# Hybrid encoder block: weight blocks of the value groups cast and reduced apart over a second load queue, and filter and forward-transform products in float32r parts

## Chip, core and metric

The kernel runs on one core of a Trainium2 chip. The metric is the time of one execution on the device, in microseconds (us). A difference below about 0.2% can't be told from no change.

## The reference

One layer on x of 512 positions by 2048 channels, in float32:

```
mod = silu(c) @ w_ada + b_ada            # shift1, scale1, gate1, shift2, scale2, gate2: 6 x 2048
h   = x * (1 + scale1) + shift1
z   = h @ w_in + b_in                    # 2048 x 9216: u, v | Hyena v, x1, x2 | gates a, b
A   = gelu(u) * (W_s @ LN(gelu(v)) + b_s)          # per chunk of 128 positions, 8 groups
B: z_h = short_conv3(z_h); v, x1, x2 = split(z_h)  # 3 x 1024 channels
   y = v
   for n, gate in enumerate((x1, x2)):             # two long convolutions
       y = gate * (irfft(rfft(y, 2L) * spectrum(filter_n)) + y * skip_n)
mix = (sigmoid(a) * (A @ w_a) + sigmoid(b) * (B @ w_b)) @ w_o + b_o
x   = LN(alpha * x + gate1 * mix)
x   = LN(alpha * x + gate2 * (relu(x * (1 + scale2) + shift2) @ w1 + b1)**2 @ w2 + b2)
```

The filters come from a small network: two sines, a product with `w3`, an exponential window. Forward and backward filter together form one two-sided kernel, whose spectrum multiplies that of the signal.

## The kernel before

**Dense products.** Every weight matrix is stored as blocks of 128 x 1024 float32 (512 KB), each holding two slices of 128 inputs by 512 outputs. A block is loaded into one of three `wraw` buffers (`Weights.load`, L120), cast by ScalarE (ACT) to float32r as `whi` (L76), and VectorE (DVE) takes the remainder `wlo` = `wraw` - `whi` (L77). The activations are kept as the same kind of pair. A product is three float32r matmuls, high by high, high by low and low by high (L187), so a block costs 24 matmuls of 128x512. A column group of 512 outputs over 2048 inputs is 8 blocks. `Weights.prepare` (L140) emits cast and remainder together and asks for the next load on SyncE's queue (SP); `take` (L153) calls it ahead of each block, so that one or two blocks are ready ahead of TensorE (PE).

The program is emitted in the order of the Python code, and every engine and queue works through its own part strictly in that order. An instruction that waits holds everything behind it on its engine.

**Start and filters.** SP's queue is asked first for `cond` (c broadcast to all partitions), then for blocks of `w_ada`; ScalarE's queue for the small tables of the filter network (L221 to L224). The rows of `w_ada` lie on partitions, and one step `ada.step` (L263) on DVE multiplies a block of 128x1024 by silu(c) and sums along the row. A slice of 128 of the modulation's shift1 and scale1 takes 4 such steps; `first_input` (L423) then makes one slice of the input pair `h1`: two sums on GpSimd (POOL), two activations on ACT (L428, L429), the remainder on POOL (L430). All of `h1` is 64 steps. A step also asks for the next `w_ada` block; nine or so are in buffers or under way.

Meanwhile the filters' spectra are made in eight parts `n` (L494). For each: `taps(n+1)`, four float32 products of the network's last layer with `w3` (L387, and L389 for the skip term in every second part); `transform(n)`, six float32 products with a table `fwd` of cosines and sines (L321, L325, L333); on DVE two `ada` steps, four products with the window (L397), and six sums (`sums`, L337 to L342). The spectra go to device memory (`store`, L401), apart from those of one convolution half, which stay.

**The value groups.** The loop of L516 computes column groups 4 and 5 of `w_in` (the Hyena `v`) together, slice by slice, since `h1` comes only as fast as the `ada` steps. Per pass `kp` of eight it prepares blocks, runs `ada` steps in fours until `h1` is three slices ahead (`LEAD`), and then runs one block of each group on PE. It is the order of this loop that sets how DVE, ACT, POOL and SP follow each other. I call it the value stage.

**Convolutions.** Column groups 6 to 9 give the gates x1 and x2. Between their blocks the convolutions run as `stages`, a table that says after which block which piece is emitted: transposes to tokens (`to_tokens`, L535), forward transforms (`Conv.odd`, L550, and `Conv.even`, L565, eight float32 products of 128x512 per convolution half and eight sums or more on DVE), six products with the spectrum per quarter (`times`, L577), folds (L587), the inverse (L613, L622). `into`, `between`, `out_of` and `last` (L642 to L677) are these tables. There are two convolutions of two halves of 512 channels each. A ring of eight PSUM banks serves all products.

After that come the remaining groups of `w_in`, `w_b`, `w_a`, `w_o` and the MLP, which the change leaves alone.

## Time and profile before

| | us |
|---|---|
| median of 3 runs | 2764.24 (2763.06 to 2766.48) |
| profiled execution | 2763.92 |
| its span in the trace | 2762.1 |
| start, to the first windowed filter part | 0 to 30.6 |
| filter parts | 30.6 to 98.7 |
| value stage on PE | 98.65 to 212.6 |
| groups 6 to 9, gates and convolutions | 212.6 to about 500 |
| the rest | to 2762.1 |

The page gives busy time per engine, queues and groups of instructions. In a row of a timeline the columns are start, duration, engine, line, operation, output and inputs, the number of instructions joined in the row, and in brackets the idle time ahead with what ended it. In a row of waits they are who waited, for whom, us in total, times, and the longest. In a row of stretches each engine's busy time is followed by its instruction count in brackets, and then come the clock that TensorE was granted, the share of the DMA engines, and GB/s.

### The profile page before, as it was taken

The numbers are of one execution on the slowest core, as the hardware profiler recorded it, in microseconds if no ns is written. First come the engines' busy times: TensorE is split into PE (matmuls) and PEld (weight loads), VectorE is DVE, ScalarE is ACT, GpSimd is POOL, SyncE is SP. The second block draws the span as 40 slices with busy tenths as digits, with TensorE's granted clock in tenths as the row PEclk, the third lists the DMA queues.
The fourth block names the chain that finished last, engine by engine and source line by source line (L and its number), as shares of the span: only waits on it lengthen the run. The fifth ranks groups of instructions, "written<-read, shape, count | busy, mean of one in ns | idle before, by whom it ended". The sixth has DMA issues, their size and how long they took to land.

```text
span 2762.1 us, 29764 instructions
## 1 busy us (share of the span) xinstructions
PE 2703.0 (98%) x11917; PEld 2199.8 (80%) x11917; DVE 1519.6 (55%) x2026; ACT 768.4 (28%) x932; POOL 109.3 (4%) x104
## 2 busy tenths in 40 slices
PE   7989999999999999999999999999999999999996
PEld 3667777888888888887988888888888888888885
DVE  7866968644566657546774343343433433434348
ACT  2234322322222222314631221312213122131232
POOL 1120000000000000050020000000000000000001
PEclk9989999999999999999999999999999999999998
DMA  8672332555665568454552222332222232223242
GB/s 321 241 293 82 127 102 99 190 193 191 201 207 191 185 202 287 139 185 163 167 163 96 99 92 101 98 99 94 97 99 94 97 99 98 94 92 107 93 143 77
DMA packets 120474, 400.46 MB, mean 145 GB/s; under 512 B 14219, under 2 KB 14315, under 8 KB 120208
## 3 DMA queue, kind: packets, MB, share of 16 engines
q1 hardware_dynamic: 119880, 398.20, 42.4%
q8 instruction: 93, 1.52, 0.2%
q10 hardware_dynamic: 456, 0.37, 0.0%
q14 instruction: 45, 0.37, 0.0%
HBM read 388.01 MB, written 10.50 MB: 144 GB/s over the span
## 4 chain that ended last, share of the span: by engine, by line
PE 88%; DVE 4%; DMA 1%; ACT 1%; issue 1%; POOL 0%; SPq 0%; DVEq 0%; ACTq 0%
PE d L187 56%; PE t L874 28%; PE inv L628 1%; DVE wlo L77 1%; PE inv L616 0%; DMA araw<-in_ada 0%; DMA wraw<-in_w_m 0%; DVE r L1026 0%; DVE r L890 0%; PE tr L539 0%; DVE r L1028 0%; PE h2T L914 0%; PE mix L750 0%; PE f L558 0%; PE f L556 0%
## 5 line engine op out<-in xcount | busy, mean ns | idle before, releaser
L187 PE MATMUL d<-act,whi 128*128 128x512 f32 (+1 forms) x4224 | 1285.1, 387 | 15.9 <-POOL act L430 9.0
L77 DVE TENSOR_TENSOR wlo<-wraw,whi 128x1024 fp32r<-128x1024 f32 x480 | 590.3, 1233 | 1030.7 <-ACT whi L76 1027.7
L76 ACT CAST whi<-wraw 128x1024 fp32r<-128x1024 f32 x480 | 504.5, 1054 | 1534.6 <-PE d L187 919.2
L187 PEld LDWEIGHTS d<-act,whi 128*128 128x128 f32 x4224 | 786.7, 189 | 181.3 <-POOL act L430 10.7
L187 PE MATMUL d<-act,wlo 128*128 128x512 f32 (+1 forms) x2112 | 811.9, 384 | 1.8 <-DVE wlo L77 1.8
L187 PEld LDWEIGHTS d<-act,wlo 128*128 128x128 f32 x2112 | 398.5, 189 | 81.7 <-DVE wlo L77 3.5
L874 PE MATMUL t<-whi,fh 128*128 128x512 f32 x960 | 373.4, 389 | 0.0
L874 PE MATMUL t<-wlo,fh 128*128 128x512 f32 x960 | 373.4, 389 | 0.0
L874 PE MATMUL t<-whi,fl 128*128 128x512 f32 x960 | 373.4, 389 | 0.0
L263 DVE SCALAR_TENSOR_TENSOR araw<-araw,cond 128x1024 f32<-128x1024 f32 x192 | 230.3, 1219 | 11.0 <-DMA araw<-in_ada 10.9
L874 PEld LDWEIGHTS t<-whi,fh 128*128 128x128 f32 x960 | 180.2, 188 | 37.5
L874 PEld LDWEIGHTS t<-wlo,fh 128*128 128x128 f32 x960 | 180.2, 188 | 37.4
L874 PEld LDWEIGHTS t<-whi,fl 128*128 128x128 f32 x960 | 180.2, 188 | 37.4
L874 PE MATMUL t<-whi,act 128*128 128x512 f32 x512 | 160.9, 393 | 0.0
L874 PEld LDWEIGHTS t<-whi,act 128*128 128x128 f32 x512 | 96.8, 189 | 20.4
L889 DVE TENSOR_TENSOR gated<-t,cond 128x512 f32<-128x512 f32 x126 | 86.2, 684 | 31.6 <-PE t L874 31.6
L874 PE MATMUL t<-wlo,act 128*128 128x512 f32 x256 | 100.4, 392 | 2.1 <-DVE wlo L77 2.1
L890 DVE TENSOR_TENSOR r<-r,gated 128x512 f32<-128x512 f32 x126 | 87.2, 692 | 4.4
L187 PE MATMUL d<-whi,act 128*128 128x512 f32 x256 | 79.0, 389 | 0.0
L984 DVE TENSOR_TENSOR relu<-relu 128x512 f32<-128x512 f32 (+1 forms) x68 | 45.6, 671 | 38.2 <-ACT fh L983 38.2
L1028 POOL TENSOR_TENSOR r<-r,ln2b 128x512 f32<-128x512 f32 x6 | 10.0, 1662 | 1306.0 <-DVE r L1026 1304.7
L874 PEld LDWEIGHTS t<-wlo,act 128*128 128x128 f32 x256 | 48.5, 189 | 12.3 <-DVE wlo L77 2.5
(220 smaller groups left out, 1886.1 us busy)
## 6 DMA issues: line engine op xcount, KB each, us to landing
wraw<-in_w_m SPq DMA_DIRECT2D x264, 512.0 KB, 3.4
araw<-in_ada SPq DMA_DIRECT2D x192, 512.0 KB, 4.9
wraw<-in_w_in SPq DMA_DIRECT2D x144, 512.0 KB, 3.5
wraw<-in_w_o SPq DMA_DIRECT2D x48, 512.0 KB, 3.9
spec<-spec SPq DMA_DIRECT2D x48, 256.0 KB, 4.0
wraw<-in_w_b SPq DMA_DIRECT2D x16, 512.0 KB, 3.6
wraw<-in_w_a SPq DMA_DIRECT2D x16, 512.0 KB, 3.9
xT<-in_xT SPq DMA_DIRECT2D x16, 256.0 KB, 6.4
```

The costliest lines, as they stand in the source:

```text
L76: nc.scalar.copy(hi, src)
L77: nc.vector.tensor_tensor(lo, src, f32(hi), op=OP.subtract)
L187: nc.tensor.matmul(out[i], a, b, start=first and m == 0, stop=last and m == 2)
L263: nc.vector.scalar_tensor_tensor(raw, raw, 1.0, cond[:, 1024 * h:1024 * (h + 1)], op0=OP.mult, op1=OP.mult, accum_out=dots[:, m, kc, h:h + 1])
L628: nc.tensor.matmul(ps[:, cl * P:(cl + 1) * P], conv.y[cl][cs][:, s], ic(4 * cs + COLUMN[cl]), start=(cs == 0), stop=(cs == 1))
L874: nc.tensor.matmul(out[i], a, b, start=kc == 0 and m == 0, stop=kc == 2 * pairs - 1 and m == 2)
L889: nc.vector.tensor_tensor(x, ps[i], g2_row[c], op=OP.mult)
L890: nc.vector.tensor_tensor(r[i][c], r[i][c], x, op=OP.add)
L984: nc.vector.tensor_tensor(x, x, x, op=OP.mult)
L1028: eng.tensor_tensor(x, x, ln2_b[c], op=OP.add)
```

## The change

Four things are changed.

1. In `Weights`, cast and remainder can be emitted apart (`cast`, `finish`), and a load asked for later (`later`, `flush`). From the filter parts to the end of the value stage the weight blocks are loaded over ScalarE's queue. The loop of the value stage goes by 16 half passes `u` of one block each: ask for the loads held back, 3 or 4 `ada` steps, the remainder of the next block, PE's block, the cast of the one after. All 64 `ada` steps are done by the thirteenth half pass.
2. The filters' last layer (`taps`) and the convolutions' forward transforms (`angle_product`) use float32r pairs in three matmuls in place of one float32 product. Pairs are made of `w3`, of the second sine's output `a2`, of the table `fwd` (after the value stage), and of the tokens. The filter parts' own transforms stay in float32.
3. The tables of stages move some pieces by one block (`late`, and `even(0)` of the second convolution into the next group).
4. At the start, the first two small tables are asked for on SP's queue, `cond` comes in two loads, the +1 on the scales moves from POOL to DVE, and 38 transposes of the identity into a bank that nothing reads (`busy`) are put on PE between the first products.

The order of the instructions moves at three places on which the prediction rests. In the rows, a name's number tells its buffers apart.

First, VectorE in the value stage, about a third of the way through. `wlo` are remainders of weight blocks, `araw` the `ada` steps. Before:

```order
L77 TENSOR_TENSOR wlo_1005<-wraw_842,whi_1004 128x1024
L77 TENSOR_TENSOR wlo_1035<-wraw_912,whi_1034 128x1024
L263 SCALAR_TENSOR_TENSOR araw_874,dots_106<-araw_874,cond_88 128x1024
L263 SCALAR_TENSOR_TENSOR araw_946,dots_106<-araw_946,cond_88 128x1024
L263 SCALAR_TENSOR_TENSOR araw_949,dots_106<-araw_949,cond_88 128x1024
L263 SCALAR_TENSOR_TENSOR araw_952,dots_106<-araw_952,cond_88 128x1024
L263 SCALAR_TENSOR_TENSOR araw_964,dots_106<-araw_964,cond_88 128x1024
L263 SCALAR_TENSOR_TENSOR araw_967,dots_106<-araw_967,cond_88 128x1024
L263 SCALAR_TENSOR_TENSOR araw_970,dots_106<-araw_970,cond_88 128x1024
L263 SCALAR_TENSOR_TENSOR araw_1042,dots_106<-araw_1042,cond_88 128x1024
L77 TENSOR_TENSOR wlo_1101<-wraw_942,whi_1100 128x1024
```

After the change:

```order
L169 TENSOR_TENSOR wlo_922<-wraw_823,whi_921 128x1024
L289 SCALAR_TENSOR_TENSOR araw_837,dots_104<-araw_837,cond_84 128x1024
L289 SCALAR_TENSOR_TENSOR araw_840,dots_104<-araw_840,cond_84 128x1024
L289 SCALAR_TENSOR_TENSOR araw_877,dots_104<-araw_877,cond_84 128x1024
L169 TENSOR_TENSOR wlo_978<-wraw_874,whi_977 128x1024
L289 SCALAR_TENSOR_TENSOR araw_880,dots_104<-araw_880,cond_84 128x1024
L289 SCALAR_TENSOR_TENSOR araw_891,dots_104<-araw_891,cond_84 128x1024
L289 SCALAR_TENSOR_TENSOR araw_894,dots_104<-araw_894,cond_84 128x1024
L289 SCALAR_TENSOR_TENSOR araw_936,dots_104<-araw_936,cond_84 128x1024
L169 TENSOR_TENSOR wlo_1025<-wraw_933,whi_1024 128x1024
```

Two remainders and then eight steps in a row have become one remainder after every three or four steps.

Second, SyncE's queue near the start of the value stage, where `wraw` are the weight blocks and `xT` the input slices. Before:

```order
L71 DMA wraw_661<-in_w_in 128x1024
L71 DMA wraw_699<-in_w_in 128x1024
L71 DMA wraw_729<-in_w_in 128x1024
L71 DMA araw_732<-in_ada 128x1024
L71 DMA araw_735<-in_ada 128x1024
L71 DMA araw_738<-in_ada 128x1024
L71 DMA araw_741<-in_ada 128x1024
L71 DMA xT_749<-in_xT 128x512
L71 DMA araw_752<-in_ada 128x1024
```

After the change:

```order
L71 DMA araw_783<-in_ada 128x1024
L71 DMA araw_786<-in_ada 128x1024
L71 DMA araw_789<-in_ada 128x1024
L71 DMA araw_826<-in_ada 128x1024
L71 DMA xT_834<-in_xT 128x512
L71 DMA araw_837<-in_ada 128x1024
L71 DMA araw_840<-in_ada 128x1024
L71 DMA araw_877<-in_ada 128x1024
L71 DMA araw_880<-in_ada 128x1024
```

And ScalarE's own order there, which now holds those loads:

```order
L71 DMA wraw_780<-in_w_in 128x1024
L164 CAST whi_820<-wraw_615 128x1024
L71 DMA wraw_823<-in_w_in 128x1024
L476 ACTIVATE act5_830<-xT_663,mod_105 128x512
L477 ACTIVATE xT_663<-xT_663,mod_105 128x512
L164 CAST whi_871<-wraw_780 128x1024
L71 DMA wraw_874<-in_w_in 128x1024
L476 ACTIVATE act6_884<-xT_768,mod_105 128x512
```

The weight blocks have left the queue in which they stood ahead of the `w_ada` blocks; they stand now between ScalarE's casts and activations.

Third, TensorE's products for the first filter part. Before:

```order
L387 MATMUL flt_197<-w3_124,a2_181 128x512
L389 MATMUL flt_197<-skip_126,first_tap_98 128x512
L387 MATMUL flt_200<-w3_124,a2_181 128x512
L387 MATMUL flt_202<-w3_124,a2_181 128x512
L387 MATMUL flt_204<-w3_124,a2_181 128x512
```

After the change, starting with the 28 transposes that `busy` puts ahead of it:

```order
L264 MATMUL busy_177<-ident_99 128x128 x14
L264 MATMUL busy_218<-ident_99 128x128 x14
L435 MATMUL flt_245<-w3h_198,a2eh_210 128x512
L435 MATMUL flt_245<-w3l_199,a2eh_210 128x512
L435 MATMUL flt_245<-w3h_198,a2el_211 128x512
L437 MATMUL flt_245<-skip_124,first_tap_96 128x512
L435 MATMUL flt_250<-w3h_198,a2eh_210 128x512
```

One float32 product with `w3` has become three with its parts; the skip term (L389, now L437) stays as it was.

```diff
+        def reload(self):
+
+            if self.later is None:
+                self.load()
+            else:
+                self.later.append(self.load)
+
+        def flush(self):
+            while self.later:
+                self.later.pop(0)()
...
-            load(raw, w[cg, kp])
+            load(raw, w[cg, kp], self.queue)
...
-                raw, what = self.raw.pop(0)
-                hi, lo = self.tiles(what)
-                split(raw, hi, lo)
-                self.ready.append((hi, lo, what))
-                self.load()
+                self.cast()
+                self.finish()
+        def cast(self):
+            raw, what = self.raw.pop(0)
+            hi, lo = self.tiles(what)
+            nc.scalar.copy(hi, raw)
+            self.half.append((raw, hi, lo, what))
+
+        def finish(self):
+            raw, hi, lo, what = self.half.pop(0)
+            nc.vector.tensor_tensor(lo, raw, f32(hi), op=OP.subtract)
+            self.ready.append((hi, lo, what))
+            self.reload()
...
-    hw1 = cload("hw1", (EMB, HID), nc.scalar)
-    featT = load(slot("featT")[:EMB], t["featT"], nc.scalar)
+    hw1 = cload("hw1", (EMB, HID))
+    featT = load(slot("featT")[:EMB], t["featT"])
+    cond = const.tile([P, D], F32, name="cond")
+    for h in range(2):
+        c_ = slice(1024 * h, 1024 * (h + 1))
+        load(cond[:, c_], t["c"][:, c_].broadcast_to([P, 1024]))
     hcol = cload("hcol", (P, 3), nc.scalar)
     hw2 = cload("hw2", (HID, P), nc.scalar)
-    cond = const.tile([P, D], F32, name="cond")
-    for h in range(4):
-        c_ = slice(512 * h, 512 * (h + 1))
-        load(cond[:, c_], t["c"][:, c_].broadcast_to([P, 512]))
...
+    def busy(n):
+
+        ps = bank("busy")
+        for _ in range(n):
+            nc.tensor.transpose(ps[:, :P], ident, ident)
...
+    def angle_product(ps, k, x, first=True, last=True):
+
+        if not isinstance(x, tuple):
+            nc.tensor.matmul(ps, fc(k), x, start=first, stop=last)
+            return
+        h, l = fc_parts
+        for m, (a, b) in enumerate(((h, x[0]), (h, x[1]), (l, x[0]))):
+            nc.tensor.matmul(ps, a(k), b, start=first and m == 0, stop=last and m == 2)
...
-            nc.tensor.matmul(ee, fc(4 * self.cs), self.src[0], start=True, stop=True)
+            angle_product(ee, 4 * self.cs, self.src[0])
...
-                    nc.tensor.matmul(o, fc(k), self.src[2 * i + 1], start=(i == 0), stop=(i == 1))
+                    angle_product(o, k, self.src[2 * i + 1], i == 0, i == 1)
...
-            even, odd = slot("a2"), slot("a2")
-            nc.scalar.activation(even, x, AF.Sin)
-            nc.scalar.activation(odd, x, AF.Sin, scale=sign)
-            self.a2 = [a.rearrange("h (p k) -> h k p", k=4) for a in (even, odd)]
+            nc.scalar.activation(x, x, AF.Sin)
+            even, odd = slot_pair("a2e"), slot_pair("a2o")
+            split(x, *even)
+            for a, b in zip(even, odd):
+                nc.scalar.activation(b, f32(a), AF.Identity, scale=sign)
+            self.a2 = [[a.rearrange("h (p k) -> h k p", k=4) for a in pair] for pair in (even, odd)]
...
+        def parts(self, n):
+            if PARTS[n][2] == 0:
+                w, skip = self.raw.pop(0)
+                both = slot_pair("w3")
+                split(w, *both)
+                self.w.append((*both, skip))
...
-            if cs == 0:
-                self.w = self.raw.pop(0)
-            w, skip = self.w
+            wh, wl, skip = self.w[0] if cs == 0 else self.w.pop(0)
+            ah, al = self.a2[cs]
             for cl in range(4):
                 ps = bank("flt")
                 extra = cs == 0 and cl == 0
-                nc.tensor.matmul(ps, self.a2[cs][:, cl, :], w, start=True, stop=not extra)
+                for m, (a, w) in enumerate(((ah, wh), (ah, wl), (al, wh))):
+                    nc.tensor.matmul(ps, a[:, cl, :], w, start=m == 0, stop=m == 2 and not extra)
                 if extra:
                     nc.tensor.matmul(ps, first_tap, skip, start=False, stop=True)
                 self.ps.append(ps)
...
     fc = table("fwd", 3)
     for m in (1, 4):
-        nc.gpsimd.tensor_scalar(bada[:, m], bada[:, m], 1.0, None, op0=OP.add)
+        nc.vector.tensor_scalar(bada[:, m], bada[:, m], 1.0, None, op0=OP.add)
+    busy(14)
     ada_steps(2)
+    flt.parts(0)
     flt.ready()
+    busy(14)
     x_load()
     for _ in range(5):
         ada.load()
     flt.taps(0)
     ada_steps(2)
     flt.windowed(0)
+    weights.later, weights.queue = [], nc.scalar
     for n in range(8):
         if n < 6 and n % 2 == 0:
             flt.fetch(n + 2)
@@ -500,43 +553,64 @@
         ada_steps(2)
         if n < 7:
             flt.windowed(n + 1)
-            flt.store()
+        flt.store()
+        if n < 6:
+            flt.parts(n + 2)
         sums()
-        if 4 <= n < 7:
+        if 2 <= n < 5:
             weights.load()
+        if n == 5:
+            weights.cast()
         if n == 6:
-            weights.prepare()
+            weights.finish()
+            weights.cast()
...
-    LEAD = 3
     ps_v = [], []
     two = [dense_steps(ps, t["w_in"], 4 + i, 8, h1) for i, ps in enumerate(ps_v)]
     yv = []
-    for kp in range(8):
-        weights.prepare()
-        while len(h1) < min(KC, 2 * kp + 2 + LEAD):
-            ada_steps(4)
-        for i, group in enumerate(two):
-            next(group)
-            if kp == 7:
-                next(group, None)
-                yv.append(short_conv(ps_v[i], 0, i))
-        if kp == 1:
+    first, steps = len(done), 64 - len(done)
+    for u in range(16):
+        kp, i = u // 2, u % 2
+        weights.flush()
+        ada_steps(min(steps, (u + 1) * steps // 13) - len(done) + first)
+        weights.finish()
+        next(two[i])
+        if kp == 7:
+            next(two[i], None)
+            yv.append(short_conv(ps_v[i], 0, i))
+        weights.cast()
+        if u == 2:
             flt.store()
             bin_c = cload("bin", (P, 72))
             hcw = cload("hcw", (P, 24, 4))
             cb = const.tile([P, 24], F32, name="cb")
-        if kp == 4:
+        if u == 8:
             nc.vector.tensor_tensor(cb, hcw[:, :, 1], bin_c[:, 16:40], op=OP.mult)
             nc.vector.tensor_tensor(cb, cb, hcw[:, :, 3], op=OP.add)
-
-
+    weights.finish()
+    weights.flush()
+    weights.later, weights.queue = None, nc.sync
+
+
+    fc_parts = [], []
+    for x in fc.tiles:
+        both = slot_pair("fc")
+        split(x, *both)
+        for p_, y in zip(fc_parts, both):
+            p_.append(y)
+    fc_parts = [columns_of(p_) for p_ in fc_parts]
...
+    def to_tokens(src, cl, dst, parts=False):
         ps = bank("tr")
         for i in range(4):
             nc.tensor.transpose(ps[:, i * P:(i + 1) * P], src[i].rearrange("c (p k) -> c k p", k=4)[:, cl, :], ident)
+        if parts:
+            dst.append(slot_pair("tok"))
+            split(ps, *dst[-1])
+            return
...
-                nc.tensor.matmul(three, fc(4 * cs + 3), self.u[3], start=True, stop=True)
+                angle_product(three, 4 * cs + 3, self.u[3])
...
-        dst.append(gate)
+        dst[cl] = slot_pair("tok")
+        split(gate, *dst[cl])
...
+    def into(conv, src, late=0):
+
+        out = {1: [do(to_tokens, src, cl, conv.u, True) for cl in range(2)],
+               2: [do(to_tokens, src, cl, conv.u, True) for cl in range(2, 4)]}
+        rest = [[do(conv.odd)], [do(conv.even, 0), do(conv.fetch, 0)], [do(conv.even, 1), do(conv.fetch, 1)],
+                [do(conv.times, 0), do(conv.fetch, 2)], [do(conv.times, 1), do(conv.fetch, 3)]]
+        out.update({3 + late + k: fs for k, fs in enumerate(rest[:5 - late])})
+        return out
+
+    def between(conv, late=0):
+
+        rest = [[do(conv.times, 1), do(conv.fetch, 3)]] * late
+        rest += [[do(conv.times, 2)], [do(conv.times, 3)], [do(conv.fold, 0)], [do(conv.fold, 1)], [do(conv.fold, 2)]]
+        return dict(enumerate(rest))
...
-                4: [lambda: [inverse(conv.y, cl, dst[cl], got) for cl in (1, 3)], lambda: after.u.extend(dst)],
-                6: [do(after.odd)], 7: [do(after.even, 0)]}
+                4: [lambda: [inverse(conv.y, cl, dst[cl], got) for cl in (1, 3)], lambda: after.u.extend(got[cl] for cl in range(4))],
+                6: [do(after.odd)]}
...
-    yx1 = short_conv(dense(t["w_in"], 7, 8, h1, stages=merged(between(c1[0]), into(c1[1], yv[1]))), 1, 1)
+    yx1 = short_conv(dense(t["w_in"], 7, 8, h1, stages=merged(between(c1[0]), into(c1[1], yv[1], 1))), 1, 1)
...
-        return {1: [do(conv.even, 1), do(conv.fetch, 0)], 2: [do(conv.times, 0), do(conv.fetch, 1)],
+        return {0: [do(conv.even, 0)], 1: [do(conv.even, 1), do(conv.fetch, 0)], 2: [do(conv.times, 0), do(conv.fetch, 1)],
```

33 lines of the change are left out of this document (14 added, 19 removed).

## The prediction

> **What bounds the kernel now.** I read the page's busy times first, then TensorE's waits in the first fifth of the span, then busy time by stretches.
>
> ```profile
> PE 2703.0 (98%) x11917; PEld 2199.8 (80%) x11917; DVE 1519.6 (55%) x2026; ACT 768.4 (28%) x932; POOL 109.3 (4%) x104
> PE d L187 <- POOL act L430: 9.0, 5, 2.0
> PE flt L387 <- ACT a L363: 6.1, 1, 6.1
> ...
> PE d L187 <- ACT act L428: 2.7, 3, 0.9
> ...
> 30.50:95.30 64.80, 64.80 (x149) 33.83 (x148) 59.76 (x99) 10.90 (x16) 4.98 (x9) 1.00 0.66 243
> 98.65:212.60 113.95, 98.59 (x387) 76.84 (x386) 81.32 (x124) 41.34 (x51) 29.24 (x36) 0.93 0.78 289
> 262.00:352.00 90.00, 90.00 (x387) 70.29 (x387) 87.55 (x125) 30.65 (x42) 0.00 (x0) 1.00 0.33 112
> 440.00:2762.00 2322.00, 2296.41 (x10422) 1910.86 (x10420) 1178.67 (x1523) 632.64 (x751) 67.03 (x44) 1.00 0.41 137
> 1521.42 87.04 PE d L187 x384
> ```
>
> TensorE sets the time nearly everywhere, so a faster piece elsewhere is worth nothing unless TensorE waits for it. It waits at the start and in the value stage, from 98.65 to 212.60. That stage is 16 blocks of 24 matmuls, 384 in all. The last row, a piece of the chain of waits in the MLP, shows what 384 such matmuls take undisturbed: 87.04. The stage takes 113.95, so 26.9 us lie open there: 15.4 idle (113.95 - 98.59), the rest at a mean granted clock of 0.93. In the filter stretch TensorE is full, but VectorE has 59.76 of 64.80; from 262 to 352 VectorE is nearly full beside a full TensorE.
>
> **The two prices of a product.** The filter parts show float32, the value stage float32r.
>
> ```profile
> 33.13 1.02 PE L321 MATMUL f_ee<-flt,fwd 128*128 128x512 f32 x2
> 33.99 1.02 PE L325 MATMUL f_eo<-flt,fwd 128*128 128x512 f32 x2
> ...
> 145.34 0.39 PE L187 MATMUL d<-act,wlo 128*128 128x512 f32 x1
> 145.57 0.62 PE L187 MATMUL d<-act,whi 128*128 128x512 f32 x2
> 146.03 0.39 PE L187 MATMUL d<-act,wlo 128*128 128x512 f32 x1
> ```
>
> From start to start a float32 product takes 33.99 - 33.13 = 0.86, three float32r matmuls 146.03 - 145.34 = 0.69 (0.68 in the 87.04 for 128 threes). Each product exchanged saves TensorE 0.18.
>
> **Start.** Before, the first windowed part is done at 30.6.
>
> ```profile
> 19.34 0.43 DVE L294 TENSOR_SCALAR sine<-sine 128x512 f32<-128x512 f32 x1
> 19.80 0.63 ACT L363 ACTIVATE a<-sine 128x512 f32<-128x512 f32 x1 [4.57 <-DVE sine L294]
> 20.49 2.09 PE L387 MATMUL flt<-w,a 128*128 128x512 f32 x2 [6.07 <-ACT a L363]
> 22.51 2.07 PE L389 MATMUL flt<-skip,first_tap 1*128 1x512 f32 x2
> 29.90 0.69 DVE L397 TENSOR_TENSOR flt<-flt,win 128x512 f32<-128x512 f32 x1 [0.86 <-PE flt L387]
> 30.51 1.21 DVE L263 SCALAR_TENSOR_TENSOR araw<-araw,cond 128x1024 f32<-128x1024 f32 x1
> 31.65 0.08 DVE L263 DVE_READ_ACCUMULATOR araw<-araw,cond 128x1 f32 x1
> 32.80 2.48 DVE L397 TENSOR_TENSOR flt<-flt,win 128x512 f32<-128x512 f32 x4
> ```
>
> The first matmuls run at half speed: 2.02 per product (22.51 - 20.49) against 0.86. The transposes are there to have TensorE at speed by then. The second sine's reduction ends at 19.77. I put it at 20.1 in the changed kernel: VectorE gains about 0.5 from the earlier tables but does the remainder of `w3` (0.6, by the 128x512 rows) and two small additions first. Then come the sine 0.63, the cast 0.6, the remainder 0.6, two `ada` steps of 1.15 (31.65 - 30.51) and four window products of 2.5, which TensorE (4 x 0.68 plus 0.9 for the skip) now precedes: 27.0. That is 3.6 earlier. Bounds: 5 if the tables come earlier still, 2 if TensorE is cold.
>
> The Trainium skill, "TensorE: Matmul & The Clock Gate", Part 4, says that transposes don't count as busy for the clock and don't release it. No row here shows transposes on a cold TensorE; by this rule `busy` does nothing.
>
> **Filter parts.** The 32 products of `taps` save 32 x 0.18 = 5.8 on TensorE, but VectorE takes over as the bound. Its busy time was 59.76 from window to the seventh set of sums; three more remainders of `w3` add 1.8, and I allow 0.8 for handovers: 62.4 for 64.80, a gain of 2.4. Bounds: 61.6 with no handovers, 66.6 if VectorE's idle 5.0 stays. Then the last transform: before, TensorE was the late one.
>
> ```profile
> 94.70 0.68 DVE L317 TENSOR_TENSOR spec<-bf_e,f_o 128x512 f32<-128x512 f32 x1
> ...
> 98.65 1.02 PE L187 MATMUL d<-act,whi 128*128 128x512 f32 x2
> ```
>
> VectorE ended the seventh sums at 95.3, TensorE its eighth transform at 98.65, 3.35 later. With VectorE late, four of its six products are done by then and two remain, 1.9: 1.4 less (bounds 1.6 and 0). So the value stage begins at 27.0 + 62.4 + 1.9 = 91.3.
>
> **Value stage.** Three rows show how it loses time: VectorE's eight steps in a row hold the slices, TensorE waits, and its clock falls; SP stands in front of weight blocks while `w_ada` is wanted.
>
> ```profile
> 136.11 0.51 PE L187 MATMUL d<-act,whi 128*128 128x512 f32 x1 [0.90 <-ACT act L428]
> 138.62 0.66 PE L187 MATMUL d<-act,whi 128*128 128x512 f32 x1 [2.00 <-POOL act L430]
> 139.50 1.05 PE L187 MATMUL d<-act,whi 128*128 128x512 f32 x2
> 140.78 1.05 PE L187 MATMUL d<-act,whi 128*128 128x512 f32 x2
> ...
> 104.82 7.79 SPq L71 DMA_DIRECT2D wraw<-in_w_in  x3
> 112.66 1.88 SPq L71 DMA_DIRECT2D araw<-in_ada  x4
> ...
> GB/s 265 342 223 176 30 368 393 412 413 292 167 393 399 345 398 409 410 404 407 410 401 411 381 288 325 404 369 83 264 369 314 384 232 0 268 304 3 0 74 268
> araw<-in_ada SPq DMA_DIRECT2D x36, 512.0 KB, 8.0
> wraw<-in_w_in SPq DMA_DIRECT2D x15, 512.0 KB, 4.4
> xT<-in_xT SPq DMA_DIRECT2D x10, 256.0 KB, 6.3
> spec<-spec SPq DMA_DIRECT2D x8, 256.0 KB, 4.5
> ...
> L77 DVE TENSOR_TENSOR wlo<-wraw,whi 128x1024 fp32r<-128x1024 f32 x16 | 20.6, 1312 | 28.3 <-ACT whi L76 28.3
> L76 ACT CAST whi<-wraw 128x1024 fp32r<-128x1024 f32 x16 | 16.1, 1042 | 5.8 <-PE d L187 5.8
> L429 ACT ACTIVATE xT<-xT,mod 128x512 f32<-128x512 f32 x12 | 9.8, 814 | 0.4
> ```
>
> After 2.0 idle, three matmuls take 1.28 (140.78 - 139.50) for some 3.4 us: each such stall costs 2 to 3 us more than itself. (The GB/s row has 40 slices from 100 to 210.)
>
> The new order has no burst. Half a pass is 5.44 on TensorE (87.04 / 16) and 3.4 x 1.15 + 1.15 = 5.1 on VectorE, and slices are two half passes ahead. What remains is the transfers. From the seventh sums on, 37 `w_ada` blocks are still to be asked for, 13 weight blocks, 9 input slices and 8 spectra: (37 + 13) x 0.524 + 17 x 0.262 = 30.7 MB before the last step at the thirteenth half pass. The row shows 393 to 413 GB/s where the queue is never held; at 400 this is 76.7 us. It begins some 2.3 after the sums, since only a step frees a buffer; with about 2 to land and 2.3 for the last step and remainder, the thirteenth remainder is done 83.3 after the sums. Three half passes follow, 16.3, and about 2.4 for a cold restart: 102.0, or 100.1 counted from TensorE's start. So 113.95 becomes 100.1, a gain of 13.9. Bounds: 92 if transfers never hold it (VectorE then has a remainder, two steps and six sums at 0.62 ahead of its first step, 1.15 + 2.3 + 3.7, so TensorE still waits some 4 us at the second block), 107 at 370 GB/s with the cold spells of today.
>
> The second queue adds waits to ScalarE: a block's issue there waits for the remainder that frees its buffer, and casts and slices stand behind it. Its own work per half pass is 1.04 + 0.85 x 1.63 + 0.35 = 2.8 of 5.44 to 6.2, which is the cover; without cover each us of wait above 2.7 is one for TensorE.
>
> The Trainium skill, "Trainium Kernel Development and Optimization", Key Constraints, says that several issuing engines share the same 16 DMA engines and save only issue time. By it the queue brings no bandwidth, and the stage would gain little.
>
> **Convolutions.** 32 forward products (four halves of eight) save 32 x 0.18 = 5.8 on TensorE. VectorE gets 19 more remainders, 12 us, of which 7 fall between 212 and 330, where it has 2.5 idle of 90 at the end. The tightest place:
>
> ```profile
> 326.62 1.22 DVE L77 TENSOR_TENSOR wlo<-wraw,whi 128x1024 fp32r<-128x1024 f32 x1
> 329.51 5.50 PE d L187 x24
> ```
>
> This remainder ends 1.7 before TensorE takes its block. Over the 52 us ahead of it VectorE gets four remainders (2.6) and gives up six products of `times` (3.6), while TensorE gets 1.4 faster: 1.3 of slack is left. Three remainders of the table fall where VectorE waited 4 to 5 us per block. I take 5.0, near the full 5.8, since the slack stays above nothing; bounds 7.3 (the 1.5 us wait for a bank at 440 goes too) and a loss of 4.
>
> **Sum.** 3.6 + 2.4 + 1.4 + 13.9 + 5.0 = 26.3 off the profiled execution's 2763.92, which lies 0.3 below the median: 2737.6, so 2738. Past 500 nothing changes.
>
> **The rivals.**
>
> *The transfers are not the bound* (chance 0.17). For it: slices of 404 to 413 GB/s, and loads that start sooner. Against it: 2.5 MB per half pass in 5.44 us would be 463 GB/s. Stage 92: 2738 - 8 = 2730 or less.
>
> *VectorE becomes the bound in the convolutions* (0.15). For it: 87.55 of 90, slack 1.3. Against it: the moved pieces. The gain of 5.0 turns into a loss of up to 4: 2743 to 2747.
>
> *The transposes leave TensorE cold* (0.08). The first four products then take 4 x 1.28 + 2.0 = 7.1 for 3.6; part of it hides behind the two steps: 2.7 later, 2741. This is what the clock page's rule gives.
>
> *The change doesn't do what it says* (0.05): transfers from two queues hold each other up and the stage stays at 112: 2750. This is what the queue rule gives.
>
> *ScalarE stands still at the issues* (0.05), the rival on the other side. If each of the 16 issues holds it for a whole landing, 8.0 as the `w_ada` row has it, half a pass is 10.8 and the stage 173: 2738 + 73 = 2811. It decides from a wait of about 5.1 us each (16 x 7.9 = 126), where the stage's loss has eaten all other gains. Against it: the buffer is free one half pass earlier.
>
> *As forecast*, 0.50.
>
> **How the numbers follow.** The middle cases lie between 2730 and 2750. The first rival can go below 2726, and the last lies beyond 2752, together with half of the convolution rival's tail: 2726 to 2752 holds eight in ten. About 0.2% (5.5 us) is what a measurement here can tell. Faster by more: all but ScalarE's rival and a tail of two others, 0.93; within: 0.03; slower: 0.04.
>
> **What would show it.** Right: window products of the first part done near 27; the value stage beginning near 91 and lasting 95 to 105 with 390 GB/s or more, and VectorE's waits there on `araw`; TensorE without new waits from 212 to 500. Wrong: waits of `whi` or `wlo` on ScalarE's queue in the value stage, new waits of L187 for `wlo` after it, or a stage of 92 with no wait for `araw`.

## The result, and the profile after

The changed kernel takes **2733.95 us** (median of 4 runs, 2733.2 to 2736.25), the kernel before 2764.7 (2763.06 to 2766.48): the ratio is 0.9891 with a 95% interval of 0.9877 to 0.9905. The forecast was 2738, with a range of 2726 to 2752. The profiled executions (2733.2 and 2763.92) have spans of 2731.4 and 2762.1, and this difference of 30.7 is what is taken apart here.

The safest way is to find the same event in both traces and to compare its times. Two events behind the value stage serve: the first transposes of the first convolution, two blocks after the stage, and the last inverse transform. The view of one tile gives first and last start, of before:

```profile
L539 PE MATMUL tr<-ident,hy x64: 270/284/285, 223.3 to 395.0; 128*128 128x128 f32 x64
L628 PE MATMUL inv<-inv,fw x32: 275/275/275, 454.6 to 522.9; 128*128 128x128 f32 x32
```

and of the changed kernel, with two rows of TensorE's and VectorE's timeline at the value stage's beginning, and the row at its end:

```profile
L609 PE MATMUL tr<-ident,hy x64: 270/284/286, 203.6 to 370.7; 128*128 128x128 f32 x64
L703 PE MATMUL inv<-inv,fw x32: 275/275/276, 427.0 to 495.2; 128*128 128x128 f32 x32
```

```profile
26.85 0.69 DVE L445 TENSOR_TENSOR flt<-flt,win 128x512 f32<-128x512 f32 x1 [0.59 <-PE flt L435]
...
88.61 0.68 DVE L356 TENSOR_TENSOR spec<-bf_e,f_o 128x512 f32<-128x512 f32 x1
...
91.91 1.02 PE L207 MATMUL d<-act,whi 128*128 128x512 f32 x2
...
190.36 0.61 PE L207 MATMUL d<-act,whi 128*128 128x512 f32 x2
191.54 0.50 PE L207 MATMUL d<-act,wlo 128*128 128x512 f32 x1 [0.57 <-DVE wlo L169]
```

| Stretch | before | changed | difference | forecast |
|---|---|---|---|---|
| start, to the first windowed part done | 30.59 | 27.54 | -3.1 | -3.6 |
| filter parts, to the seventh sums done | 64.79 | 61.75 | -3.0 | -2.4 |
| from there to the value stage's first matmul | 3.27 | 2.62 | -0.7 | -1.4 |
| value stage on TensorE | 113.95 | 98.45 | -15.5 | -13.9 |
| from its end to the last inverse transform | 310.3 | 304.8 | -5.5 | -5.0 |
| the rest, the same instructions in both | 2239.2 | 2236.2 | -3.0 | 0 |

Each line of the change lies within 1.6 us of its term. The last line is a saving that no part of the change makes; it comes back at the end.

The waits of TensorE from 0 to 520 (tile and line that waited, what for, total, times, longest) answer to the rows shown of before:

```profile
PE d L207 <- DVE wlo L169: 9.4, 9, 2.6
...
PE flt L435 <- ACT a2eh L76: 3.0, 1, 3.0
```

The waits for the slices (`act`, 9.0 and 2.7 before) are gone. What TensorE waits for now is the remainder of a weight block (`wlo`) on VectorE. The busy times by stretch (length, then PE, PEld, DVE, ACT, POOL, then granted clock, DMA share, GB/s) say why:

```profile
27.46:89.21 61.75, 61.75 (x178) 37.85 (x177) 60.48 (x102) 12.79 (x19) 5.01 (x9) 1.00 0.76 284
91.91:190.36 98.45, 90.80 (x387) 71.31 (x385) 87.62 (x122) 40.29 (x50) 43.76 (x36) 1.00 0.85 327
96.00:168.00 72.00, 65.73 (x278) 51.12 (x277) 70.06 (x96) 24.35 (x28) 37.67 (x30) 1.00 1.02 401
```

In the filter parts TensorE is busy for all of 61.75, VectorE for 60.48. In the value stage the clock is 1.00 where it was 0.93. From 96 to 168 the transfers run at 401 GB/s on average, with the DMA engines busy throughout, and VectorE is busy for 70.06 of 72. Two resources are full at once, and the wait for `wlo` doesn't tell which of them is late. The timeline of VectorE and GpSimd (start, length, engine, line; in brackets the idle time ahead and what ended it) has something that the value stage of the kernel before didn't have:

```profile
105.49 1.22 DVE L289 SCALAR_TENSOR_TENSOR araw<-araw,cond 128x1024 f32<-128x1024 f32 x1
...
106.26 1.60 POOL L478 TENSOR_TENSOR act<-xT,act 128x512 fp32r<-128x512 f32 x1 [1.78 <-ACT xT L477]
106.64 2.31 DVE L289 SCALAR_TENSOR_TENSOR araw<-araw,cond 128x1024 f32<-128x1024 f32 x1
...
108.88 1.22 DVE L289 SCALAR_TENSOR_TENSOR araw<-araw,cond 128x1024 f32<-128x1024 f32 x1
```

A `w_ada` step that runs into GpSimd's low part of a slice takes 2.3 instead of 1.22. Eight of the stage's steps take 1.8 to 2.3.

### The profile page after: what moved, and what is told of

The parts are those of the page before. It is cut to its first block, busy times and chain, and to the rows that moved or that the text cites. A ratio compares the mean times of both kernels' runs of the same rounds, so it can differ in the third digit from the quotient of the medians.

```text
span 2731.4 us, 30019 instructions
## 1 busy us (share of the span) xinstructions
PE 2688.6 (98%) x12019; PEld 2210.1 (81%) x12019; DVE 1539.5 (56%) x2052; ACT 777.8 (28%) x949; POOL 118.8 (4%) x102
## 4 chain that ended last, share of the span: by engine, by line
PE 91%; DVE 5%; DMA 3%; issue 1%; ACT 1%; SPq 0%; DVEq 0%; ACTq 0%
PE d L207 57%; PE t L952 29%; DMA araw<-in_ada 2%; PE flt L435 1%; PE f_o L338 1%; DVE wlo L169 1%; DMA spec<-spec 1%; PE inv L703 1%; PE inv L690 1%; DMA wraw<-in_w_m 0%; PE f L342 0%; DVE araw L289 0%; DVE r L1104 0%; DVE r L968 0%; PE tr L609 0%
## 5 line engine op out<-in xcount | busy, mean ns | idle before, releaser
L207 PE MATMUL d<-act,whi 128*128 128x512 f32 (+1 forms) x4224 | 1273.1, 384 | 0.0
L207 PEld LDWEIGHTS d<-act,whi 128*128 128x128 f32 x4224 | 783.1, 188 | 155.6 <-issue 2.4
L207 PE MATMUL d<-act,wlo 128*128 128x512 f32 (+1 forms) x2112 | 810.2, 384 | 10.2 <-DVE wlo L169 10.2
L207 PEld LDWEIGHTS d<-act,wlo 128*128 128x128 f32 x2112 | 396.7, 188 | 93.3 <-DVE wlo L169 15.9
L289 DVE SCALAR_TENSOR_TENSOR araw<-araw,cond 128x1024 f32<-128x1024 f32 x192 | 238.6, 1259 | 7.8 <-DMA araw<-in_ada 7.6
L207 PE MATMUL d<-whi,act 128*128 128x512 f32 x256 | 79.0, 389 | 0.0
```

What stands on the lines that cost most here:

```text
L207: nc.tensor.matmul(out[i], a, b, start=first and m == 0, stop=last and m == 2)
L289: nc.vector.scalar_tensor_tensor(raw, raw, 1.0, cond[:, 1024 * h:1024 * (h + 1)], op0=OP.mult, op1=OP.mult, accum_out=dots[:, m, kc, h:h + 1])
```

## The experiments

All kernels are the changed one with an edit. The column "13th remainder" is the start of VectorE's remainder in the thirteenth half pass (the fifteenth for the two kernels marked with a star), behind which no `w_ada` step is left. Five of the kernels serve for their times alone and don't compute the layer: half_blocks, half_and_low, half_bytes and half_no_low use half of each `w_ada` block for the slices of the value stage, and no_low and half_no_low leave out the low parts of those slices.

| Kernel | stage begins | 13th remainder | first transposes | last inverse | median | ratio to before, interval |
|---|---|---|---|---|---|---|
| changed | 91.9 | 173.1 | 203.6 | 495.2 | 2733.95 | 0.9891, 0.9877 to 0.9905 |
| half_blocks | 90.6 | 178.3 | 208.8 | 500.4 | 2738.62 | 0.9911, 0.9895 to 0.9928 |
| low_on_vector | 91.8 | 175.3 | 205.8 | 497.4 | 2737.43 | 0.9904, 0.9889 to 0.9919 |
| half_and_low | 91.9 | 176.6 | 207.1 | 498.7 | 2737.72 | 0.9906, 0.9891 to 0.992 |
| half_bytes | 90.5 | 173.3 | 203.9 | 495.5 | 2733.91 | 0.9892, 0.9878 to 0.9907 |
| no_low | 90.5 | 173.8 | 204.3 | 495.9 | 2734.6 | 0.9896, 0.9881 to 0.991 |
| half_no_low | 90.5 | 163.7 | 196.6 | 488.2 | 2727.44 | 0.9868, 0.9853 to 0.9882 |
| one_queue | 91.7 | 173.6 | 204.1 | 495.7 | 2736.43 | 0.9901, 0.9886 to 0.9916 |
| steps_15 | 91.8 | 174.9* | 200.8 | 492.4 | 2731.33 | 0.9882, 0.9865 to 0.9898 |
| busy_to_taps | 92.8 | 175.1 | 205.6 | 497.2 | 2736.99 | 0.9903, 0.9889 to 0.9918 |
| taps_f32 | 93.1 | 175.3 | 205.8 | 497.5 | 2736.96 | 0.9893, 0.9876 to 0.9909 |
| conv_f32 | 90.5 | 172.4 | 202.9 | 500.6 | 2741.15 | 0.9916, 0.9901 to 0.9931 |
| best | 90.0 | 174.5* | 196.6 | 488.2 | 2727.8 | 0.9868, 0.9852 to 0.9885 |

**What bounds the value stage: transfers or VectorE?** The first attempt took three kernels. In half_blocks `part` is 512 in the value stage; in low_on_vector a list keeps the slice, and VectorE subtracts three steps later.

```diff
# half_blocks
-                load(raw, t["ada"][m, kc, h])
+                load(raw[:, :self.part], t["ada"][m, kc, h][:, :self.part])
...
+            for _ in range(1024 // n):
+                nc.vector.scalar_tensor_tensor(raw[:, :n], raw[:, :n], 1.0, cond[:, 1024 * h:1024 * h + n], ...
# low_on_vector
-        nc.gpsimd.tensor_tensor(lo, xt, f32(hi), op=OP.subtract)
+        low.append((lo, xt, hi))
```

> The changed kernel, but in the value stage each w_ada block is loaded by half (512 of its 1024 columns) and its step is done twice on that half, so VectorE has about the same work and the transfers some 9 MB less of 31 (the modulation of 9 input slices comes out of half the columns). Theory A (the prediction's: the transfers, at 400 to 420 GB/s from 96 to 168, set when the thirteenth remainder is done): the stage of 98.45 us on TensorE loses what VectorE stood waiting for transfers in it, 3 us (four waits of 0.24 to 1.15 for araw and two of some 0.5 at remainders), so about 95.5, 2731 in all; then VectorE sets it, since one step in four takes 2.30 us instead of 1.21 while GpSimd computes a slice's low part. Theory B (VectorE alone sets it, the transfers only fill the time): no change, 98 to 99. Theory C (neither; TensorE's own waits at its first two half passes): no change either.

> The changed kernel, but the low part of each input slice is computed by VectorE, three steps after the slice's sums, instead of by GpSimd. The eleven steps that took 2.30 us should take 1.21, and VectorE gets twelve instructions of 0.6: 5 us less on VectorE in the value stage. Theory A (transfers set it): the stage stays at 97.5 to 98.5, since VectorE then waits longer for araw, 2.4 now and some 6 to 8 then. Theory B (VectorE sets it): the stage falls by 4 to 5, to 94, and the total to 2729. If the steps still take 2.30, the hold-up isn't GpSimd's.

> Both edits of the two kernels above: half of each w_ada block loaded and used twice, and the slices' low parts on VectorE. Theory A: neither the transfers nor VectorE is left as the bound, and the stage falls by more than the two edits do apart, to 90 to 93 (TensorE's own 87 and the wait at its second half pass), the total to 2726 to 2729. Theory B: the stage is the same as with the low parts alone.

VectorE's groups from 96 to 174 (busy time, mean ns) of the changed kernel and of these kernels, in the order changed, half_blocks, low_on_vector:

```profile
L289 DVE SCALAR_TENSOR_TENSOR araw<-araw,cond 128x1024 f32<-128x1024 f32 x44 | 59.8, 1395 | 2.6 <-DMA araw<-in_ada 2.4
```

```profile
L291 DVE SCALAR_TENSOR_TENSOR araw<-araw,cond 128x512 f32<-128x512 f32 (+1 forms) x75 | 62.8, 866 | 1.1
...
L291 DVE DVE_READ_ACCUMULATOR araw<-araw,cond 128x1 f32 x74 | 6.0, 81 | 0.0
```

```profile
L289 DVE SCALAR_TENSOR_TENSOR araw<-araw,cond 128x1024 f32<-128x1024 f32 x43 | 51.5, 1221 | 3.8 <-DMA araw<-in_ada 3.6
...
L483 DVE TENSOR_TENSOR act<-xT,act 128x512 fp32r<-128x512 f32 x11 | 7.6, 688 | 0.5 <-ACT xT L477 0.5
```

Two things follow. With the low parts off GpSimd the mean step falls from 1395 to 1221 ns and none takes 2.3: the hold-up is GpSimd's. But neither edit lifted its resource alone. Two half steps cost more than one whole, so half_blocks gave VectorE more work than it had, and it came 5.2 later with no wait for transfers left; the low parts cost VectorE 7.6 us themselves, about what the hold-ups had cost (44 x 0.174 = 7.7), and put its early work later; half_and_low, with both edits, came 3.5 later. The question stayed open, and two cleaner edits followed: in half_bytes a step is one instruction that reads its half twice, and in no_low the low part is left out.

```diff
# half_bytes
+            if n < 1024:
+                raw, c_, out = raw[:, None, :n].to_broadcast([P, 2, n]), c_.rearrange("p (a n) -> p a n", a=2), self.spare
# no_low
-        nc.scalar.activation(xt, xt, AF.Identity, bias=sh, scale=sc)
-        nc.gpsimd.tensor_tensor(lo, xt, f32(hi), op=OP.subtract)
+        nc.scalar.activation(lo, xt, AF.Identity, bias=sh, scale=sc)
```

> The changed kernel with half of each w_ada block loaded in the value stage, as before, but each step now one instruction over the half read twice, so that VectorE's time stays what it is (the output, which nothing reads, goes to a spare tile; the modulation of 9 slices comes out of half the columns). Theory A (the transfers set the thirteenth remainder, at 173.1 in the changed kernel): it starts 2 to 3 us earlier, by the 2.4 us for which VectorE stood waiting for araw; no more, because VectorE is all but full. Theory B (VectorE sets it): within 1 us of 173.1. In neither theory does halving the bytes bring the 8 us that the prediction's rival gave.

> The changed kernel without the computation of the slices' low parts on GpSimd: ScalarE writes the slice itself into the tile of the low part (so the products with the low part are wrong), GpSimd has no work on slices left, VectorE gets none. The eight steps of 2.2 to 2.3 us should take 1.2: 8.7 us less on VectorE before the thirteenth remainder, with the same bytes. Theory A: VectorE waits that much longer for araw, and the thirteenth remainder stays within 2 us of 173.1. Theory B: it starts 6 to 9 us earlier, at 164 to 167, and the stage is 90 to 92.

With the bytes halved the thirteenth remainder starts at 173.3; with VectorE relieved, at 173.8. Theory B holds in the first kernel and theory A in the second, so neither is right alone. Busy time from 96 to 168 in half_bytes, and VectorE's waits from 89.5 to 176 in no_low:

```profile
96.00:168.00 72.00, 65.08 (x271) 51.02 (x270) 71.06 (x96) 24.11 (x28) 37.69 (x30) 0.98 0.81 278
```

```profile
DVE araw L289 <- DMA araw<-in_ada: 11.4, 13, 1.8
```

At 278 GB/s the transfers are far from full, and VectorE, with 71.06 of 72, takes just as long. In no_low VectorE, relieved of its hold-ups, waits 11.4 us for transfers instead of 2.4. So both edits were put together.

> Both edits at once: half of each w_ada block loaded in the value stage and read twice, and no low part of the slices on GpSimd (ScalarE writes the slice itself there). Each alone left the thirteenth remainder within 0.7 us of 173.1. My theory now: the transfers and VectorE are two bounds of the same height, so that only both edits together bring anything: VectorE's 13 remainders, 41 steps and 6 sums without hold-ups and without waits take 13 x 1.14 + 41 x 1.15 + 3.7 = 65.7, so the thirteenth remainder comes near 160 by VectorE alone, and TensorE (12 half passes of 5.44 from 91, its stall of 3.7 and its second start: 160 to 161) is level with it: the stage ends near 179, 10 to 12 earlier, the total at 2722 to 2725. Rival: a third thing (ScalarE's order of casts and slices, the depth of the rings) holds it as well: the thirteenth remainder at 170 or later.

The thirteenth remainder starts at 163.7, 9.4 earlier than in the changed kernel. Busy time from 96 to 168:

```profile
96.00:168.00 72.00, 68.30 (x296) 56.12 (x295) 67.95 (x105) 28.29 (x35) 23.97 (x22) 0.98 0.85 294
```

TensorE's last wait in the stage is at its second half pass (3.7 us, up to 100.7), and from 110 to 180 it is busy for all of 70.0: here it is the bound itself. This shows that transfers and VectorE are two bounds of about the same height. The sizes came out 3 to 4 us smaller than expected (the stage ends at 183.3, not at 179).

**The second queue.**

```diff
-    weights.later, weights.queue = [], nc.scalar
+    weights.later, weights.queue = [], nc.sync
```

> The changed kernel with the value stage's weight blocks issued on SP's queue like everything else, in the new order. SP then stands at w_ada blocks whose buffer isn't free before it comes to a weight block, at most one half pass late. My theory: the order, not the queue, brought most of the 15.5 us; the stage gets 0 to 4 us longer (98.5 to 102.5), the total 2734 to 2738. Rival: the second queue is what keeps the transfers full; then SP's stops come back (7.8 us for three weight blocks in the kernel before), GB/s falls to 370 or less in the stage, which takes 105 or more. The Trainium skill, Trainium Kernel Development and Optimization, Key Constraints, says that a second issuing engine saves issue time only: by it the stage stays at 98.5.

The stage takes 99.2 instead of 98.45 (204.1 less 13.24, as in the changed kernel, and less 91.66), and the transfers run as fast:

```profile
96.00:168.00 72.00, 67.04 (x281) 52.86 (x280) 68.59 (x97) 24.68 (x29) 35.66 (x30) 0.98 1.03 401
```

With 401 GB/s on one queue and on two, the second one is worth 0.7 us here, and the rest of the 15.5 us comes with the new order, which spreads the steps and issues a block's cast, remainder and load apart. No run puts the old order back, so which part of the new one brings how much stays open. (Of the 3.2 us between the two profiled executions, 2.6 lie past the last inverse transform, where the instructions are the same.) The Trainium skill's rule (Trainium Kernel Development and Optimization, Key Constraints: several issuing engines share the 16 DMA engines) agrees with this pair; the prediction's rival, which took the rule to mean a stage of 112, was wrong because the gain didn't come from the queue.

**Where the steps end.**

```diff
-        ada_steps(min(steps, (u + 1) * steps // 13) - len(done) + first)
+        ada_steps(min(steps, (u + 1) * steps // 15) - len(done) + first)
```

> One number changed: the remaining w_ada steps are spread over 15 half passes of the value stage instead of 13. If the stage's end is the time of the last step (bound by transfers and VectorE together, wherever in TensorE's order it falls) plus the half passes of 5.4 us that come after it, then 15 leaves one half pass after it where there were three: 10.9 less, given back in part by two more remainders on VectorE and two more weight blocks on the way ahead of the last step (1.1 to 1.3 each) and by a wait of 1 to 3 us for the last slice, which is ready 6.5 after its last step: 5 to 8 us shorter, a stage of 90 to 93, a total of 2726 to 2729. Rival: the last slices come too late, TensorE waits 5 or more for GpSimd at the fifteenth half pass and goes cold: no change, 2734.

The first transposes come 2.8 earlier and the median is 2.6 lower, about half of the least that was expected. TensorE's waits from 96 to 200 name the rival as the reason, at the thirteenth half pass instead of the fifteenth:

```profile
PE d L207 <- DVE wlo L169: 3.2, 3, 1.5
PE d L207 <- POOL act L478: 2.0, 1, 2.0
PE d L207 <- ACT act L476: 1.7, 1, 1.7
```

With the steps spread thinner, a slice is not ready when its half pass begins. With thirteen the slices have slack, which is paid for with half passes behind the last step.

**The start.**

```diff
     flt.ready()
-    busy(14)
+    busy(36)
```

> The last group of transposes with 36 instead of 14, so that TensorE works until the taps' first operand is there (it stood idle for 3.0 us ahead of them, ran the first three matmuls at 0.25 apart and the next fourteen at 0.43). If transposes keep the clock up, the taps run at 0.24 throughout, the first windowed part is done 1.5 to 2.5 us earlier, at 25 to 26, and the total falls by as much. By the Trainium skill, TensorE: Matmul and the clock gate, Part 4, transposes don't count as work for the clock: by it nothing changes, and the taps are at 0.43 as before.

Timeline of the changed kernel at the start:

```profile
4.96 2.39 PE L264 MATMUL busy<-ident 128*128 128x128 f32 x10
...
12.31 4.27 PE L264 MATMUL busy<-ident 128*128 128x128 f32 x28
19.60 0.62 PE L435 MATMUL flt<-w3h,a2eh 128*128 128x512 f32 x1 [3.03 <-ACT a2eh L76]
20.06 0.40 PE L435 MATMUL flt<-w3l,a2eh 128*128 128x512 f32 x1
20.33 0.62 PE L435 MATMUL flt<-w3h,a2el 128*128 128x512 f32 x1
...
23.63 0.63 PE L435 MATMUL flt<-w3h,a2el 128*128 128x512 f32 x1
24.05 0.63 PE L435 MATMUL flt<-w3h,a2eh 128*128 128x512 f32 x1
```

and of busy_to_taps, with the cast and the remainder of the second `w3`:

```profile
12.44 7.79 PE L264 MATMUL busy<-ident 128*128 128x128 f32 x50
...
22.97 0.40 PE L435 MATMUL flt<-w3h,a2eh 128*128 128x512 f32 x1
23.21 0.40 PE L435 MATMUL flt<-w3l,a2eh 128*128 128x512 f32 x1
...
33.19 0.62 ACT L76 CAST w3h<-w 128x512 fp32r<-128x512 f32 x1 [4.35 <-DMA w<-in_w]
33.84 0.69 DVE L77 TENSOR_TENSOR w3l<-w,w3h 128x512 fp32r<-128x512 f32 x1 [3.02 <-ACT w3h L76]
```

The profile merges the transposes into rows; one by one, the 50 of busy_to_taps start 0.21 us apart up to 16.8 and 0.11 apart from there on. Ahead of that change TensorE did nothing but transposes for 4.4 us (12.44 to 16.8), so transposes do bring the clock up. Behind them the taps are 0.24 apart, those next to a float32 product excepted. In the changed kernel the transposes come to 0.11 apart as well, but 3.0 us of idleness follow, and 1.6 us after work has resumed, at 21.2, the granted clock falls to 0.50 and stays there to 28.0: the taps go from 0.27 to 0.43. The clock from 18 to 26 (the eighth figure) of the changed kernel, then of busy_to_taps:

```profile
18.00:26.00 8.00, 6.40 (x13) 3.92 (x14) 5.03 (x9) 4.27 (x6) 1.50 (x3) 0.70 1.03 408
```

```profile
18.00:26.00 8.00, 8.00 (x42) 7.00 (x41) 6.63 (x11) 4.28 (x6) 1.49 (x3) 1.00 1.03 408
```

The Trainium skill, "TensorE: Matmul & The Clock Gate", Part 4, says that transposes don't engage the full clock; these runs don't bear that out. But the time didn't fall: the windowed part was done 2.3 earlier (25.3), and VectorE then stood 3.0 us before the second `w3`, whose transfer, asked for behind `w_ada` blocks, lands at 33. The value stage begins 0.9 later than in the changed kernel, and the median is 3.0 higher. Neither theory had the transfer that bounds the start; the last kernel of this section asks for it earlier and begins the stage 1.9 sooner.

```diff
# taps_f32: one float32 product for a tap, as before the change
-                for m, (a, w) in enumerate(((ah, wh), (ah, wl), (al, wh))):
-                    nc.tensor.matmul(ps, a[:, cl, :], w, start=m == 0, stop=m == 2 and not extra)
+                nc.tensor.matmul(ps, self.a2[cs][:, cl, :], w, start=True, stop=not extra)
```

> The changed kernel with the taps of the filters back in float32 (one product each, no parts of w3 or of the sines; start, order and queues as changed). In the changed kernel TensorE worked without a wait from 30.1 to 91.9, and VectorE waited some 1.5 us between the first windowed part and the seventh sums. If TensorE bounds the filter parts, as this says, 28 products cost it 0.61 per four more (8.58 against 7.97 from one transform to the next in the two kernels): 4.3 later at the value stage's first matmul, 95 to 96, and 2738 in all. If VectorE bounds them, as the prediction had it, it loses three remainders of 0.6 and the stage begins where it did, 90.5 to 92, 2734 in all.

Neither number came out: the stage begins at 93.1, 1.2 later than in the changed kernel. The timeline of taps_f32 splits this in two:

```profile
18.42 1.25 PE L429 MATMUL flt<-w,a 128*128 128x512 f32 x2 [1.16 <-ACT a L402]
...
32.56 1.22 PE L429 MATMUL flt<-w,a 128*128 128x512 f32 x2 [0.37 <-DMA w<-in_w]
```

The third part's taps begin at 32.56 here and at 34.83 in the changed kernel; from there to the stage it is 60.56 against 57.08. So float32r saves 3.5 us in the repeated parts, as a TensorE bound should give, and costs 2.3 at the start: the cast and the remainder of the sine put the first tap at 19.60 instead of 18.42, and the longer idleness (3.0 us instead of 1.2) costs TensorE its clock, which taps_f32 keeps. Float32 for the first two parts alone would take both; it was not tried.

**The convolutions.**

```diff
# conv_f32: no parts of the table, the columns and the gated values
-    fc_parts = [columns_of(p_) for p_ in fc_parts]
...
-        dst[cl] = slot_pair("tok")
-        split(gate, *dst[cl])
+        dst[cl] = gate
```

> The changed kernel with the convolutions' forward transforms back in float32 (one product each, no parts of the table, of the columns or of the gated values; the moved pieces stay where the change put them). The prediction's term: 32 products at 0.18 more are 5.8 on TensorE, less what the remainders of the parts cost it: the wait of 2.7 at the first two blocks after the value stage stays, since short_conv makes it and not the parts. So 5 to 6 us longer from the stage's end to the last inverse transform (304.8 in the changed kernel, 190.4 to 495.2), 2739 to 2740 in all. Rival: the parts cost as much as they bring, 0 to 2 us.

From 13.24 before the first transposes to the last inverse transform it takes 310.9, against 304.8: 6.1 us longer, as expected. What else the change does in this stretch makes it 0.6 longer (310.9 against 310.3 in the kernel before).

**Putting it together.**

```diff
-        mod_sum(slice(0, 2), kc, nc.gpsimd)
+        mod_sum(slice(0, 2), kc, nc.vector if kc >= 12 else nc.gpsimd)
...
-    busy(14)
+    busy(32)
     x_load()
+    flt.fetch_w(2)
     for _ in range(5):
         ada.load()
...
-        ada_steps(min(steps, (u + 1) * steps // 13) - len(done) + first)
+        ada_steps(min(steps, (u + 1) * steps // 15) - len(done) + first)
...
+        if kp == 7:
+            weights.finish()
+            yv.append(short_conv(ps_v[i], 0, i))
```

> Five small edits on the changed kernel: the steps spread over 15 half passes (2.8 us in the run of that edit alone); transposes up to the taps (which then ran at 0.24 apart, and gained nothing since VectorE stood 3.0 us before the second w3, whose transfer landed at 33); so that second w3 asked for ahead of five w_ada blocks; the remainders of the two blocks after the stage put ahead of the short convolutions on VectorE (TensorE waited 1.8 for them, 2.7 with the clock); the sums of the last four slices on VectorE instead of GpSimd (TensorE waited 2.0 for a slice in the run with 15). If these places are what they look like, 1.5 to 2 from the start, 2.8, 2.7 and 1 to 2 add up to 8 to 9.5: 2724 to 2727. If the start only shifts the value stage's transfers, 2727 to 2729.

2727.8 (2726.8 to 2729.04), ratio to before 0.9868 (0.9852 to 0.9885). The interval overlaps that of the changed kernel, its times don't, and the last inverse transform comes 7.0 earlier: 1.9 from the start, 2.7 inside the stage and 2.4 from the two blocks behind it, where TensorE has no wait left. The fifth edit, the sums of the last slices on VectorE, brought nothing that shows: TensorE waits 5.3 us for those slices, where it waited 3.7 in steps_15.

```profile
PE d L207 <- POOL act L484: 4.3, 2, 2.6
PE d L207 <- DVE wlo L169: 1.6, 1, 1.6
PE d L207 <- ACT act L482: 1.0, 1, 1.0
```

## Why the prediction was right, and where only its number was

**Start** (3.6 forecast, 3.1 measured): two errors that cancel. The second sine's reduction was put at 20.1 and ended at 18.24 (its last row is 17.81 + 0.43). The assumption that TensorE is at speed for the taps failed: the transposes did warm it, the 3.0 us of idleness behind them lost it again. The rival "the transposes leave TensorE cold" had the result half right for another reason. And behind both lay a transfer, the second `w3` (cast at 32.2 here, at 33.2 in busy_to_taps), that no step of the working looked at.

**Filter parts** (2.4, 3.0): the step "VectorE takes over as the bound" failed. From 30.08 to 91.91 TensorE worked without a wait, and taps_f32 shows the 3.5 of a TensorE bound. That its 2.4 came near the 3.0 was luck. The price was off as well: four products exchanged brought 0.61, 0.15 each instead of 0.18, because three float32r matmuls take 0.71 here (eleven matmuls in 2.59 us, 79.43 to 82.02), not the 0.68 of the value stage. The rows of the changed kernel:

```profile
75.77 3.60 PE L338 MATMUL f_o<-flt,fwd 128*128 128x512 f32 x8
78.80 0.80 PE L435 MATMUL flt<-w3h,a2oh 128*128 128x512 f32 x1
79.43 0.40 PE L435 MATMUL flt<-w3l,a2oh 128*128 128x512 f32 x1
79.67 0.40 PE L435 MATMUL flt<-w3h,a2ol 128*128 128x512 f32 x1
...
82.02 1.02 PE L338 MATMUL f_ee<-flt,fwd 128*128 128x512 f32 x2
```

and of before:

```profile
80.17 1.02 PE L321 MATMUL f_ee<-flt,fwd 128*128 128x512 f32 x2
...
88.75 1.02 PE L321 MATMUL f_ee<-flt,fwd 128*128 128x512 f32 x2
```

From one transform to the next (74.05 to 82.02) that is 7.97; before, 80.17 to 88.75, it was 8.58. (The first float32r matmul behind a float32 one stands at 0.63 in these rows, but the transform ahead of it, 74.05 to 78.80, is as much shorter: 4.75 against 5.14.) The handover (1.4, measured 0.7) rested on the same step: since VectorE isn't late, three of TensorE's six products were still to come (2.62 at 0.86 each), not two.

**Value stage** (13.9, 15.5): the size held, the reason was half of the truth. Counted from the seventh sums the forecast was 102.0 and 101.1 came. The thirteenth remainder was to be done 83.3 after the sums by transfers alone, and was done after 85.0; the cold restart of 2.4 behind it didn't come. The step that failed is "5.1 on VectorE" per half pass: it left out that a step beside GpSimd's low part takes up to 2.3, 7.7 us in all, and with them VectorE needs as long as the transfers (half_bytes: 173.3 at 278 GB/s instead of 401). The rival "the transfers are not the bound" was wrong in the same place: without the transfers' limit the stage doesn't become 92, it stays near 100 (100.1 in half_bytes: 203.86 less 13.24 and 90.49). Only with both lifted (half_no_low) does it come to 92.8 (183.3 less 90.5). The Trainium skill, "SBUF — State Buffer", Who interferes with whom, has the missing rule: a VectorE instruction with two SBUF inputs contends with a GpSimd instruction that reads SBUF, and whichever starts second is blocked. The trace agrees, with 2.31 against 1.22. In the value stage of the kernel before, with its bursts of eight steps, no step took more than 1.48, so the rows used couldn't show the price. Other rows of that trace could: at 1190.08 a remainder `wlo` of 128x1024 that begins 0.04 us behind a GpSimd instruction on two tiles takes 2.32.

**ScalarE's rival**: didn't occur. Issuing a weight block takes ScalarE 0.33, and in the stage it waits for the slices' sums on GpSimd and VectorE, hardly for a transfer.

**Convolutions** (5.0, 5.5): right in size. The 32 products with their remainders bring 6.1 net (conv_f32), where the products alone were put at 5.8, so no cost of the remainders shows. The sign that was to speak against the forecast, new waits of L207 for `wlo`, did appear, at the two blocks behind the stage, and cost 2.4 (13.24 from the stage's end to the transposes for two blocks of 5.44). Their cause isn't the new remainders, for conv_f32 has none of these and still takes 13.24 there; it is the eight instructions of `short_conv` that now stand ahead of each on VectorE: with the order turned round (best) the waits are gone. A bank's wait of 1.5 that went at the same time hid part of them in the sum.

**Past 500** (0, 3.0): the instructions are the same, and the forecast was right about the change and wrong about the difference. Busy time by stretches of before, then of the changed kernel (the eighth figure is the granted clock):

```profile
1250.00:1300.00 50.00, 48.44 (x206) 39.47 (x207) 31.76 (x41) 16.96 (x17) 0.00 (x0) 0.97 0.55 186
2700.00:2749.00 49.00, 39.98 (x177) 32.77 (x175) 43.78 (x75) 10.32 (x17) 9.97 (x6) 0.94 0.15 55
```

```profile
1222.00:1271.00 49.00, 47.11 (x208) 38.63 (x209) 32.37 (x42) 17.17 (x18) 0.00 (x0) 1.00 0.56 192
2669.50:2718.50 49.00, 41.19 (x182) 33.79 (x180) 43.40 (x74) 10.29 (x17) 9.99 (x6) 0.96 0.15 56
```

After the same short waits TensorE lost its clock for a while in the one execution and not in the other. In the profiled executions of the twelve edited kernels this rest took between 2235.7 and 2238.9, and the granted clock sorts them. Counting these two as well, eight executions have a spell of 3.4 us at half clock between 1216 and 1255, and the rest takes 2237.8 to 2239.2 in them; six have none there, and it takes 2235.7 to 2236.6. Why the spell comes in some executions and not in others stays open; the instructions are the same. Of the 30.7, then, 27.7 are the change's, against the 26.3 of the sum.

## What to carry to other kernels

When two resources are nearly full in a stage, lift each of them in a kernel of its own and then both: an edit that brings nothing doesn't say that its resource isn't a bound. Price an instruction by a row in which its neighbours on the other engines are those that it will have in the new order, for one that moves beside another engine's work can double. And compare the times of one event in both traces before comparing totals: here 3 us of scatter lay in instructions that the change doesn't touch.
